# Eight gate tiles instead of four in the block of seven products, four instead of eight as fillers, and the low halves of their weights on GpSimd

## The chip, the core and the metric

The kernel runs on one core of a Trainium2 chip. The metric is the device time of one execution in microseconds (us), the median of three runs. The profile is one further execution of the same program. Engines are called as in the profile: PE (TensorE), DVE (VectorE), ACT (ScalarE), POOL (GpSimd), SP (the queue that issues most DMAs).

## What is computed

One encoder layer on 512 tokens of width 2048, in float32. One input projection gives queries, keys, values and gates of two groups of 16 heads (group A: dilated sliding windows with a bucketed bias; group B: neighbourhoods on an 8 by 64 grid). The attention outputs are multiplied by SiLU of the gates, projected once, added to a scaled input and normalised:

```python
h = jnp.einsum('bsd,de->bse', x, w_in[layer])
qa, ka, va, ga, qb, kb, vb, gb = jnp.split(h, splits, axis=-1)
ya = _dilated_attention(heads(qa, N_HEADS_A), heads(ka, N_HEADS_A), heads(va, N_HEADS_A), t5_bias)
yb = _neighbourhood_attention(heads(qb, N_HEADS_B), heads(kb, N_HEADS_B), heads(vb, N_HEADS_B), na_rpb[layer])
ya = merge(ya) * jax.nn.silu(ga.astype(jnp.float32))
yb = merge(yb) * jax.nn.silu(gb.astype(jnp.float32))
y = jnp.concatenate([ya, yb], axis=-1).astype(x.dtype)
out = jnp.einsum('bse,ed->bsd', y, w_out[layer])
x = _layer_norm(DEEPNORM_ALPHA * x + out, ln_gain[layer], ln_bias[layer])
```

The gates have 2048 columns, cut into sixteen tiles of 128 columns.

## The kernel before, in words

Every product of float32 matrices is made of three matmuls. Each operand is split into a high half, which is its copy rounded to the matmul's type (`wh`, by ACT), and a low half, which is what is left (`wl` = raw - high, by DVE); PE adds high by high, high by low and low by high.

The work runs in five stages.

1. `plain_block` computes the first `EARLY` = 4 gate tiles while the input is loaded and split.
2. `run_blocks` computes the projections of q, k and v by Strassen's scheme: a product of 2 by 2 blocks by seven products instead of eight. There are six such blocks of 28 "jobs" (7 products by 4 units). A job has four parts, issued at fixed distances: add two raw weight pieces (DVE, L371), high half (ACT, L375), low half (DVE, L380), 12 matmuls of 512 columns (PE, L402 to L404). After the fourth block stands one more block, of kind "s", for `MID` = 4 gate tiles. There the weights are the stationary side and the tokens the moving side, cut into halves of 256 tokens, so its matmuls have 256 columns (L393 to L395); it has 14 jobs of 24 such matmuls.
3. The remaining eight gate tiles and half of the output projection are "fillers": matmuls handed out one at a time by a generator. A gate tile is 48 filler matmuls of 512 columns (L561); the first half of the output projection (`out_first`, L755) is 384 more. 49 fillers run before attention starts.
4. Attention is a loop over 136 steps n, four for each of 32 heads, on the order written in the code. Heads go in pairs of group A and pairs of group B. A step makes the scores of 128 queries (PE L665 and L666), adds the bias and takes the minimum `mn` (DVE `s`, L622), takes exponentials with their sums (ACT, L626); two steps later the probabilities are transposed (PE L685 into `pt`) and split into `th` (ACT, L690) and `tl` (DVE, L691). In step n % 4 = 2 the previous head's values are multiplied in (PE L707 into `pv`: first `th`, then `tl`), and its two halves are added by way of a copy `tmp` (ACT L831) into `y` (DVE L832). Between these stand the fillers: `amount` of them in each of the four steps of a head, 8+6+1+6 = 21 up to step 63, 8+7+1+7 = 23 after that. For each pair of heads, DVE also multiplies `y` by the gates (L730) and by the reciprocal of the sums (L738) and makes the low half of `yk` (L740); the reciprocals go through memory on POOL's queue (L721, L723).
5. The second half of the output projection and the normalisation.

The fillers' weights are loaded by SP (L540) into a ring of four, asked for one piece ahead (`prepare`), split one step later (ACT L546) and two steps later (DVE L547), and used 24 matmuls at a time. The filler generator may only reach a part of `out_first` when the `yk` tile that it multiplies has been made, two for each quarter of the weights.

The order on PE, SP, DVE and ACT in stages 2 to 4 is that of the code; POOL's order is set by a scheduler.

Of the kernel before, what the change touches and what calls it, by code (L numbers as in the profile page):

```python
# [25 lines left out]
HALF = 256  # L26
# [38 lines left out]
ORDER = [(m % 2, m // 2) for m in range(2 * PAIRS)]  # L65
EARLY, MID = 4, 4
BIAS = ((0, 24), (192, 32), (448, 24))
# [3 lines left out]
def hybrid_layer(tc, xT, xn, w_in, w_early, w_mid, w_gate, w_out, t5x, brow, rpb, cmask, eye, gain, lbias, out):  # L71
    nc = tc.nc
    from contextlib import ExitStack
    with ExitStack() as ctx:
# [275 lines left out]
        def strassen_block(src, kind, g, hooks):  # L350

            base = len(jobs)
            units, tiles = (2, 1) if kind == "s" else (4, 2)

            def load(q, tags):
                def run():
                    for u in range(units):
                        raw = slot(tags[u], F32, "braw")
# [6 lines left out]
            def product(i, pool, q, other=None, onto=None):  # L365
# [7 lines left out]
                def high(u):  # L373
                    h = halves.next("wh", F32R)
                    nc.scalar.activation(h, raws[q][u], AF.Copy)  # L375
                    return h

                def low(u, h):
                    l = halves.next("wl", F32R)
                    nc.vector.tensor_tensor(l, raws[q][u], f(h), ALU.subtract)  # L380
                    return h, l

                def run(u, h, l):
                    if u == 0 and first:
                        accs.extend(bank(pool, "acc") for _ in range(tiles))
                    if kind == "s":
                        for kk in range(4):
                            k = 4 * u + kk
                            ah, al = operand(i, k)
                            for n in range(2):  # L390
                                c = slice(256 * kk + 128 * n, 256 * kk + 128 * n + 128)
                                o = accs[0][:, HALF * n:HALF * n + HALF]
                                nc.tensor.matmul(o, h[:, c], ah, start=first and k == 0 and n == 0, stop=False, skip_group_check=skip)  # L393
                                nc.tensor.matmul(o, h[:, c], al, start=False, stop=False, skip_group_check=skip)
                                nc.tensor.matmul(o, l[:, c], ah, start=False, stop=k == 7 and n == 1, skip_group_check=skip)  # L395
                    for t in range(2 if kind != "s" else 0):
# [24 lines left out]
            def pair(name):  # L421
                if name not in made:
                    t = temps.next(name)
                    made[name] = [t[:, :512], t[:, 512:]]
                return made[name]
# [46 lines left out]
            def put(name, ch, half, t):  # L472
                o = p1[t] if name == "c11" else pair(home[name])[t]
                if kind == "v":
                    store_v(g, ch, half, t, o)
                    return
                sg = vst.next("sg")[:, :512]
                silu(sg, o)
                for n in range(2):
                    nc.sync.dma_start(sg_d[EARLY + 2 * ch + n][:, HALF * half:HALF * half + HALF], sg[:, HALF * n:HALF * n + HALF])  # L480

# [54 lines left out]
        def prepare():  # L536

            while stream and len(raws) < 4:
                raws.append(raw_ring.next("wraw"))
                nc.sync.dma_start(raws[-1], stream.pop(0))  # L540
            if not raws:
                return
            raw = raws.pop(0)
            h, l = halves.next("wh", F32R), halves.next("wl", F32R)
            ready.append((h, l))
            later(1, lambda: nc.scalar.activation(h, raw, AF.Copy))  # L546
            later(2, lambda: nc.vector.tensor_tensor(l, raw, f(h), ALU.subtract), True)  # L547

# [256 lines left out]
        with tc.manual_schedule(engines=engines):  # L805
# [212 lines left out]
def _weights(w_in, w_out):  # L1018
# [20 lines left out]
    for i in range(2):  # L1039
        for j in range(2):  # L1040
            a = np.concatenate([w[8 * i:8 * i + 8, :, c:c + 128] for c in gate[EARLY + 2 * j:EARLY + 2 * j + 2]], axis=2)
            mid.append(a.reshape(2, 4, 128, 256).transpose(0, 2, 1, 3).reshape(2, 128, 1024))
    return (np.concatenate(blocks), early, np.concatenate(mid), np.concatenate([narrow(c) for c in gate[EARLY + MID:]]),
# [37 lines left out]
```

## Time and profile before

| | us |
|---|---|
| median of three runs | 976.12 (976.05 to 976.37) |
| the profiled execution, whole | 976.42 |
| its span, first to last instruction | 974.6 |
| block "s" (first to last of its matmuls) | 367.9 to 409.0 |
| first filler, first score matmul, last score matmul | 563.1, 576.4, 869.4 |

Busy shares over the span are PE 99%, DVE 78%, ACT 51%, POOL 18%. A matmul's record includes the time until its result has landed, and matmuls overlap, so PE's price for one is the distance between the starts of two neighbours and not the duration in the record. A row of a view by stretches gives the stretch, its length, and for each engine the busy time and, in brackets, the number of instructions; then the clock granted to PE, the DMA engines' busy share and their rate. A row of the view by instructions in time gives start, duration, engine, line, operation, output<-input, shape and count, and in square brackets the idle time ahead with what ended it.

### The profile page before, as it was taken

Reading aid. Unit: us, or ns where it says so; the run is one execution under the profiler, and the core shown is the slowest. Engines: PE = TensorE matmul, PEld = TensorE weight load, DVE = VectorE, ACT = ScalarE, POOL = GpSimd, SP = SyncE. Lnnn points to the kernel's source line nnn. Section 1 sums busy time; section 2 is a strip of 40 time slices with the busy share of each in tenths; the row PEclk is TensorE's granted clock in tenths of the full one; section 3 lists DMA queues with packets and bytes.
Section 4 is the critical chain, followed back from the end, with each engine's and each line's share of the span. In section 5 each row is a group of like instructions: output and inputs, shape, how many; then the busy total and the mean of one; then the engine's idle time right before and its main releaser. Section 6 shows DMA issues by size and latency. Waiting matters only on the chain.

```text
span 974.6 us, 13969 instructions
## 1 busy us (share of the span) xinstructions
PE 964.0 (99%) x4779; PEld 804.2 (83%) x4779; DVE 758.6 (78%) x1143; ACT 497.1 (51%) x858; POOL 176.5 (18%) x325
## 2 busy tenths in 40 slices
PE   8999999999999999999999999999999999999996
PEld 6887888888888889988888888888888888888885
DVE  7897778679789777796788856777876767777877
ACT  7454444444444344443445446767766666763300
POOL 1006646835642000000000000011110000100021
PEclk9999999999999999999999999999999999999998
DMA  9816796698496087420872687878877688768222
GB/s 332 280 65 133 225 329 213 171 308 220 115 334 226 22 283 204 163 96 21 265 183 96 205 273 213 226 224 228 233 229 222 195 236 214 203 223 298 87 72 102
DMA packets 119287, 194.17 MB, mean 199 GB/s; under 512 B 48479, under 2 KB 68831, under 8 KB 119216
## 3 DMA queue, kind: packets, MB, share of 16 engines
q1 hardware_dynamic: 106544, 169.67, 57.0%
q0 software_dynamic: 12096, 22.95, 8.7%
q8 instruction: 38, 0.62, 0.3%
q10 hardware_dynamic: 576, 0.66, 0.2%
q14 instruction: 33, 0.27, 0.1%
HBM read 148.68 MB, written 44.50 MB: 198 GB/s over the span
## 4 chain that ended last, share of the span: by engine, by line
PE 96%; DVE 1%; ACT 1%; DMA 1%; issue 0%; SPq 0%; DVEq 0%; ACTq 0%
PE acc L402 16%; PE acc L404 16%; PE acc L403 16%; PE acc L755 15%; PE acc L561 9%; PE pv L707 4%; PE pt L685 4%; PE sc L666 2%; PE sc L665 2%; PE pt L259 1%; PE acc L278 1%; PE acc L279 1%; PE acc L280 1%; PE sc L755 1%; PE acc L393 1%; PE acc L395 1%
## 5 line engine op out<-in xcount | busy, mean ns | idle before, releaser
L375 ACT ACTIVATE wh<-braw 128x1024 fp32r<-128x1024 f32 x182 | 193.3, 1062 | 268.6 <-PE acc L403 201.4
L380 DVE TENSOR_TENSOR wl<-braw,wh 128x1024 fp32r<-128x1024 f32 x182 | 222.7, 1226 | 52.4 <-ACT wh L375 52.1
L402 PE MATMUL acc<-wh,xk 128*128 128x512 f32 x384 | 151.5, 394 | 0.0
L404 PE MATMUL acc<-wl,xk 128*128 128x512 f32 x384 | 149.9, 390 | 0.0
L403 PE MATMUL acc<-wh,xk 128*128 128x512 f32 x384 | 149.7, 390 | 0.0
L371 DVE TENSOR_TENSOR braw<-braw 128x1024 f32<-128x1024 f32 x104 | 127.7, 1228 | 0.1
L402 PE MATMUL acc<-wh,op 128*128 128x512 f32 x288 | 113.3, 393 | 0.0
L404 PE MATMUL acc<-wl,op 128*128 128x512 f32 x288 | 112.3, 390 | 0.0
L403 PE MATMUL acc<-wh,op 128*128 128x512 f32 x288 | 112.2, 390 | 0.0
L755 PE MATMUL acc<-wh,yk 128*128 128x512 f32 x320 | 108.2, 402 | 0.0
L691 DVE TENSOR_TENSOR tl<-pt,th 128x256 fp32r<-128x256 f32 (+1 forms) x128 | 71.1, 555 | 35.8 <-ACT th L690 34.1
L690 ACT ACTIVATE th<-pt 128x256 fp32r<-128x256 f32 (+1 forms) x128 | 62.2, 489 | 47.6 <-PE pt L685 45.4
L404 PEld LDWEIGHTS acc<-wl,xk 128*128 128x128 f32 x384 | 72.1, 188 | 15.3
L402 PEld LDWEIGHTS acc<-wh,xk 128*128 128x128 f32 x384 | 72.2, 188 | 15.2 <-ACT bias L150 0.9
L403 PEld LDWEIGHTS acc<-wh,xk 128*128 128x128 f32 x384 | 72.2, 188 | 14.4
L626 ACT ACTIVATE p<-s,mn 128x512 f32<-128x512 f32 (+1 forms) x96 | 62.2, 648 | 29.0 <-DVE mn L622 28.6
L622 DVE CUSTOM_DVE_ANT_0 s<-sc,biases 128x512 f32<-128x512 f32 (+2 forms) x128 | 67.7, 529 | 10.9 <-PE sc L666 10.0
L561 PE MATMUL acc<-xk,wh 128*128 128x512 f32 x256 | 75.3, 404 | 0.0
L755 PEld LDWEIGHTS acc<-wh,yk 128*128 128x128 f32 x320 | 58.5, 189 | 8.8
L160 POOL DMA_DIRECT2D bias<-rows_d x128 | 61.3, 487 | 16.4 <-DMA bias<-rows_d 5.3
L755 PE MATMUL acc<-wl,yk 128*128 128x512 f32 x160 | 64.0, 403 | 0.0
L404 PEld LDWEIGHTS acc<-wl,op 128*128 128x128 f32 x288 | 54.1, 188 | 11.4
(185 smaller groups left out, 1707.1 us busy)
## 6 DMA issues: line engine op xcount, KB each, us to landing
braw<-in_w_in SPq DMA_DIRECT2D x96, 512.0 KB
wraw<-in_w_out SPq DMA_DIRECT2D x32, 512.0 KB
k_d<-kst SPq DMA_DIRECT2D x64, 128.0 KB
q_d<-kst SPq DMA_DIRECT2D x64, 128.0 KB
v_d<-vst SPq DMA_DIRECT2D x32, 256.0 KB
q<-q_d SPq DMA_DIRECT2D x32, 256.0 KB
wraw<-in_w_gate SPq DMA_DIRECT2D x16, 512.0 KB
k<-k_d SPq DMA_DIRECT2D x16, 512.0 KB
```

The source lines that it names most:

```text
L371: nc.vector.tensor_tensor(raws[q][u], raws[q][u], raws[other][u], ALU.add)
L375: nc.scalar.activation(h, raws[q][u], AF.Copy)
L380: nc.vector.tensor_tensor(l, raws[q][u], f(h), ALU.subtract)
L402: nc.tensor.matmul(accs[t], ah[:, q], h[:, c], start=first and k == 0, stop=False, skip_group_check=skip)
L403: nc.tensor.matmul(accs[t], al[:, q], h[:, c], start=False, stop=False, skip_group_check=skip)
L404: nc.tensor.matmul(accs[t], ah[:, q], l[:, c], start=False, stop=k == 7, skip_group_check=skip)
L561: nc.tensor.matmul(acc, w[:, k * 128:k * 128 + 128], X[8 * u + k][:, s], start=u == 0 and n == 0 and k == 0, stop=u == 1 and n == 2 and k ...
L622: nc.vector.tensor_tensor_reduce(*flat, bias, 1.0, 3e38, ALU.add, ALU.min, mn)
L626: nc.scalar.activation(p[:, to:to + n].rearrange("p (b r c) -> p b r c", r=8, c=c), s[:, :n].rearrange(order, r=8, c=c), AF.Exp, bias=mn, ...
L690: nc.scalar.activation(th, pt[:, :nch], AF.Copy)
L691: nc.vector.tensor_tensor(tl, pt[:, :nch], f(th), ALU.subtract)
L755: nc.tensor.matmul(acc[:, part], yk[k][:, s, c], w[:, wk], start=first and kk == 0 and n == 0, stop=last and kk == 1 and n == 2)
```

## The change

`MID` goes from 4 to 8. The block "s" now has four column tiles in each half of its weights instead of two: 28 jobs of 24 matmuls of 256 columns, the same job count and the same loading scheme as the other blocks, and two accumulators for each product where it had one. Four gate tiles (192 filler matmuls, eight weight pieces of 512 KB) disappear from the fillers. The low halves of the fillers' first eight weight pieces, which are all that the four remaining gate tiles use, are subtracted by POOL in two halves of 512 columns. The fillers handed out in a head's four steps become 5+3+1+2 = 11 up to step 75 and 8+6+1+6 = 21 after that. The diff, cut:

```diff
-EARLY, MID = 4, 4
+EARLY, MID = 4, 8
...
-            units, tiles = (2, 1) if kind == "s" else (4, 2)
+            units, tiles = 4, 2
+            cols, wide = (128 * MID // 2, (512, HALF * (MID // 2 - 2))) if kind == "s" else (512, (512, 512))
...
                     if kind == "s":
-                        for kk in range(4):
-                            k = 4 * u + kk
+                        for kk in range(2):
+                            k = 2 * u + kk
                             ah, al = operand(i, k)
-                            for n in range(2):
-                                c = slice(256 * kk + 128 * n, 256 * kk + 128 * n + 128)
-                                o = accs[0][:, HALF * n:HALF * n + HALF]
-                                nc.tensor.matmul(o, h[:, c], ah, start=first and k == 0 and n == 0, stop=False, skip_group_check=skip)
+                            for n in range(MID // 2):
+                                c = slice(cols * kk + 128 * n, cols * kk + 128 * n + 128)
+                                o = accs[n // 2][:, HALF * (n % 2):HALF * (n % 2) + HALF]
+                                nc.tensor.matmul(o, h[:, c], ah, start=first and k == 0 and n % 2 == 0, stop=False, skip_group_check=skip)
...
-            if kind == "s":
-                for q, ahead, i, m in ((0, 6, 0, 0), (1, 5, 0, 2), (3, 3, 1, 0), (2, 0, 1, 2)):
-                    behind.setdefault(base - ahead, []).append(load(q, tags[i][m:m + 2]))
-            else:
-                for q, ahead, i in ((0, 6, 0), (1, 4, 1), (3, 2, 2)):
-                    behind.setdefault(base - ahead if base else -4, []).append(load(q, tags[i]))
-                at(2, 2, load(2, tags[1]))
+            for q, ahead, i in ((0, 6, 0), (1, 4, 1), (3, 2, 2)):
+                behind.setdefault(base - ahead if base else -4, []).append(load(q, tags[i]))
+            at(2, 2, load(2, tags[1]))
...
-            later(2, lambda: nc.vector.tensor_tensor(l, raw, f(h), ALU.subtract), True)
+
+            def low(n):
+                c = slice(512 * n, 512 * n + 512)
+                nc.gpsimd.tensor_tensor(l[:, c], raw[:, c], f(h[:, c]), ALU.subtract)
+
+            if len(stream) + len(raws) >= 16:
+                for n in range(2):
+                    later(2, lambda n=n: low(n))
+            else:
+                later(2, lambda: nc.vector.tensor_tensor(l, raw, f(h), ALU.subtract), True)
...
-                amount = ((8, 6, 1, 6) if n < 64 else (8, 7, 1, 7))[b]
+                amount = ((5, 3, 1, 2) if n < 76 else (8, 6, 1, 6))[b]
```

What this does to the order shows at three places. First PE in the second head of attention (a head of group A), from the scores of its step n % 4 = 2; `pv` are the previous head's values, `pt` the transposes, `acc` the fillers. Before:

```order
L665 MATMUL sc<-k,q 128x512
L666 MATMUL sc<-k,ql 128x512
L707 MATMUL pv<-th,vv 128x512 x4
L707 MATMUL pv<-tl,vv 128x512 x4
L561 MATMUL acc<-xk_110,wh 128x512
L685 MATMUL pt<-ident,p 128x128 x4
L665 MATMUL sc<-k,q 128x512
L666 MATMUL sc<-k,ql 128x512
L561 MATMUL acc<-xk_111,wh 128x512
L561 MATMUL acc<-xk_112,wh 128x512
L561 MATMUL acc<-xk_113,wh 128x512
L685 MATMUL pt<-ident,p 128x128 x4
```

The same place after the change (lines are seven higher there):

```order
L672 MATMUL sc<-k,q 128x512
L673 MATMUL sc<-k,ql 128x512
L714 MATMUL pv<-th,vv 128x512 x4
L714 MATMUL pv<-tl,vv 128x512 x4
L568 MATMUL acc<-xk_102,wh 128x512
L692 MATMUL pt<-ident,p 128x128 x4
L672 MATMUL sc<-k,q 128x512
L673 MATMUL sc<-k,ql 128x512
L568 MATMUL acc<-xk_103,wh 128x512
L692 MATMUL pt<-ident,p 128x128 x4
```

Between the scores of the next step and the transposes that follow them stands one filler instead of three; the other steps are thinned in the same way.

Second DVE, from the addition `y` in the third head (L832 before, L839 after). Before:

```order
L832 TENSOR_TENSOR y<-pv,tmp 64x512
L691 TENSOR_TENSOR tl<-pt,th 128x256
L547 TENSOR_TENSOR wl<-wraw,wh 128x1024
L622 ISA s,mn<-sc,biases 128x192
L622 ISA mn 128x1
L691 TENSOR_TENSOR tl<-pt,th 128x256
```

After:

```order
L839 TENSOR_TENSOR y<-pv,tmp 64x512
L698 TENSOR_TENSOR tl<-pt,th 128x256
L629 ISA s,mn<-sc,biases 128x192
L629 ISA mn 128x1
L698 TENSOR_TENSOR tl<-pt,th 128x256
```

The low half of a filler weight, which stood between two steps' work, is gone from DVE's line.

Third POOL, from its first instruction after the setup for attention; `sg_d` are finished gate tiles, `rc_d` and `rc` the reciprocals on their way through memory. Before:

```order
L568 DMA sg_d<-sgo 128x512
L721 DMA rc_d<-tmp 8x128
L568 DMA sg_d<-sgo 128x512
L723 DMA rc<-rc_d 64x512 x2
L721 DMA rc_d<-tmp 8x128
L723 DMA rc<-rc_d 64x512 x2
```

After:

```order
L548 TENSOR_TENSOR wl<-wraw,wh 128x512 x6
L575 DMA sg_d<-sgo 128x512
L548 TENSOR_TENSOR wl<-wraw,wh 128x512 x4
L728 DMA rc_d<-tmp 8x128
L730 DMA rc<-rc_d 64x512 x2
L548 TENSOR_TENSOR wl<-wraw,wh 128x512 x2
L728 DMA rc_d<-tmp 8x128
L575 DMA sg_d<-sgo 128x512
L730 DMA rc<-rc_d 64x512 x2
```

The subtractions now share POOL's line with the issues of those DMAs; three of the eight weight pieces come ahead of the first gate's store.

More of the change, by code (lines that the diff above doesn't have):

```diff
@@ L357, in run @@
                     for u in range(units):
[L358 removed]
+                        raw = slot(tags[u], F32, "braw")[:, :2 * cols]
                         nc.sync.dma_start(raw, src[units * q + u])
@@ L373, in high @@
                 def high(u):
-                    h = halves.next("wh", F32R)
+                    h = halves.next("wh", F32R)[:, :2 * cols]
                     nc.scalar.activation(h, raws[q][u], AF.Copy)
@@ L378, in low @@
                 def low(u, h):
-                    l = halves.next("wl", F32R)
+                    l = halves.next("wl", F32R)[:, :2 * cols]
                     nc.vector.tensor_tensor(l, raws[q][u], f(h), ALU.subtract)
@@ L423, in pair @@
                     t = temps.next(name)
-                    made[name] = [t[:, :512], t[:, 512:]]
+                    made[name] = [t[:, :512], t[:, 512:512 + wide[1]]]
                 return made[name]
@@ L476, in put @@
                     return
-                sg = vst.next("sg")[:, :512]
+                sg = vst.next("sg")[:, :wide[t]]
                 silu(sg, o)
-                for n in range(2):
-                    nc.sync.dma_start(sg_d[EARLY + 2 * ch + n][:, HALF * half:HALF * half + HALF], sg[:, HALF * n:HALF * n + HALF])
+                for n in range(wide[t] // HALF):
+                    nc.sync.dma_start(sg_d[EARLY + MID // 2 * ch + 2 * t + n][:, HALF * half:HALF * half + HALF], sg[:, HALF * n:HALF * n + HALF])
             for t in range(tiles):
```

10 lines of the change are left out of this document (6 added, 4 removed).

## Prediction

> **What bounds the kernel now.** I read the page first, then PE's groups and neighbouring starts, then the stage of attention by stretches, by groups and by waits.
>
> ```profile
> span 974.6 us, 13969 instructions
> PE 964.0 (99%) x4779; PEld 804.2 (83%) x4779; DVE 758.6 (78%) x1143; ACT 497.1 (51%) x858; POOL 176.5 (18%) x325
> PE 96%; DVE 1%; ACT 1%; DMA 1%; issue 0%; SPq 0%; DVEq 0%; ACTq 0%
> ```
>
> PE is busy for 99% of the span and holds 96% of the chain that ended last: what shortens PE's work shortens the kernel, for as long as PE stays the one that is waited for. The stage at stake is attention's first 76 steps, 19 heads, in which the change hands out fewer fillers. Its stretch runs from the first score matmul to that of step 76:
>
> ```profile
> 576.42:749.42 173.00, 172.99 (x939) 143.91 (x938) 127.25 (x299) 120.42 (x284) 17.88 (x33) 1.00 0.81 227
> 576.42:749.42 173.00, 27.56 (x76) 14.37 (x76) 1.00 0.81 227
> ```
>
> The second row counts the L665 matmuls alone: 76 steps. PE is covered for all 173.0 us, DVE works 127.25 and ACT 120.42, the DMA engines are busy 81% of the time. So in this stage DVE has 46 us to spare and ACT 53, and what they wait for costs nothing yet:
>
> ```profile
> DVE tl L691 <- ACT th L690: 20.8, 29, 1.2
> DVE y L832 <- ACT tmp L831: 19.4, 16, 1.7
> ```
>
> **The change, part by part.** It moves work between two kinds of matmul and takes cover away from attention. PE's prices first, from the starts of neighbours in the view by time:
>
> ```profile
> 570.76 3.79 PE L561 MATMUL acc<-xk,wh 128*128 128x512 f32 x16
> 369.37 0.28 PE L393 MATMUL acc<-xk,wh 128*128 128x256 f32 x1
> ...
> 371.17 0.28 PE L393 MATMUL acc<-xk,wh 128*128 128x256 f32 x1
> ```
>
> Sixteen fillers in a row take 3.79 us, of which the last one's record is 0.39, so 15 distances of 0.2267 us. Between the two L393 starts, 1.80 us apart, lie 15 distances of matmuls of 256 columns (five triples of L393 to L395), 0.120 us each: more than half of 0.2267. *Removed:* four gate tiles of 48 fillers, 192 x 0.2267 = 43.5 us. *Added:* the block "s" does 7 x 48 = 336 matmuls of 256 columns before and 672 after, 336 x 0.120 = 40.3 us. PE's work falls by 3.2 us. Counted by columns it would fall by 12,288 of 98,304, an eighth of the 43.5, 5.4 us; the narrow matmul takes 2.2 of that back.
>
> The Trainium skill's TensorE page ("TensorE: Matmul & The Clock Gate", section Back-to-back issue gap) gives an isolated matmul 262 cycles at 256 columns and 518 at 512, 109 and 216 ns. By these figures 41.4 us would go and 36.7 come, 4.7 saved instead of 3.2; the trace's 120 and 227 ns do not agree, and I use the trace.
>
> The doubled block costs the other engines nothing on the path. It becomes like the k, q and v blocks, whose 28 jobs give PE 12 x 0.2267 = 2.72 us each where these give 24 x 0.120 = 2.88; DVE and ACT do the same three passes over 1024 columns for a job in both. One of those blocks:
>
> ```profile
> 99.30:176.00 76.70, 76.70 (x355) 63.48 (x354) 59.43 (x59) 34.09 (x39) 49.20 (x101) 1.00 0.77 248
> ```
>
> PE is covered throughout with DVE at 59.43 of 76.70. Eight more pieces of 512 KB are loaded there and eight fewer in attention.
>
> *Attention, steps 0 to 75.* Before, 16 heads x 21 + 3 x 23 = 405 fillers; after, 19 x 11 = 209. That is 196 fewer, 44.4 us, so PE alone would need 173.0 - 44.4 = 128.6 us. After step 76 nearly nothing changes: 768 - 49 - 405 = 314 fillers were left before, 576 - 49 - 209 = 318 are left after, at the 21 per head under which PE was covered before. So the question is whether DVE and ACT can do the 19 heads in 128.6 us. Their savings:
>
> ```profile
> L547 DVE TENSOR_TENSOR wl<-wraw,wh 128x1024 fp32r<-128x1024 f32 x17 | 20.7, 1217 | 0.0
> L567 DVE SCALAR_TENSOR_TENSOR sgo<-sgo,acc 128x512 f32<-128x512 f32 x8 | 5.4, 678 | 0.0
> L546 ACT ACTIVATE wh<-wraw 128x1024 fp32r<-128x1024 f32 x17 | 17.8, 1049 | 0.0
> ```
>
> 17 weight pieces were split here. After, 209 fillers ask for 8 or 9; the first four pieces are asked for before step 0, the next four go to POOL in steps 8 to 37, and the rest, 4, come back to DVE. So DVE loses 13 x 1.217 = 15.8 us and four `sgo`, 2.7: 127.25 - 18.5 = 108.8 us. ACT loses 8 x 1.049 and four tanh of 0.59: 109.7 us. Both fit into 128.6, at 85%. What counts is whether their waits shrink with PE's work. Here is one step with values in a head of group A:
>
> ```profile
> 660.50 0.60 PE L685 MATMUL pt<-ident,p 128*128 128x128 f32 x4
> 660.86 0.95 PE L561 MATMUL acc<-xk,wh 128*128 128x512 f32 x3
> 661.14 0.60 ACT L690 ACTIVATE th<-pt 128x512 fp32r<-128x512 f32 x1 [0.73 <-PE pt L685]
> 661.63 0.72 ACT L626 ACTIVATE p<-s,mn 128x512 f32<-128x512 f32 x1
> 661.64 0.39 PE L665 MATMUL sc<-k,q 128*128 128x512 f32 x1
> 661.77 0.69 DVE L691 TENSOR_TENSOR tl<-pt,th 128x512 fp32r<-128x512 f32 x1 [0.62 <-ACT th L690]
> 662.11 1.07 PE L707 MATMUL pv<-th,vv 128*128 128x512 f32 x4
> 662.38 0.68 DVE L622 CUSTOM_DVE_ANT_0 s<-sc,biases 128x512 f32<-128x512 f32 x1
> 663.01 1.07 PE L707 MATMUL pv<-tl,vv 128*128 128x512 f32 x4
> 663.29 0.71 ACT L626 ACTIVATE p<-s,mn 128x512 f32<-128x512 f32 x1
> 663.92 0.39 PE L561 MATMUL acc<-xk,wh 128*128 128x512 f32 x1
> 664.12 0.59 ACT L831 ACTIVATE tmp<-pv 64x512 f32<-64x512 f32 x1
> 664.75 0.68 DVE L832 TENSOR_TENSOR y<-pv,tmp 64x512 f32<-64x512 f32 x1 [1.08 <-ACT tmp L831]
> ```
>
> `tl` ends at 662.46 and `y` starts 2.29 us later, and no filler stands between: values, the exponential after `s`, and `tmp` do. So the 19.4 us of waits for `tmp` stay whatever PE saves. The waits for `th` are of another kind: `th` itself waited for transposes that PE reached late, behind fillers, and these may shrink. If all of them go, DVE's line is 108.8 + 19.4 = 128.2 us long, as long as PE's 128.6; if none goes, 149.0.
>
> I take the middle, because a walk through one head gives it. By the durations above, in us after the end of `tl`: `y` ends at 2.98; `tl` and `s` of the next step follow, ending at 3.6 and 4.2; another `tl` and `s` end at 4.8 and 5.4; the exponential, begun at 4.3, is read out at 5.1, the `th` behind it ends at 5.7, and the third `tl` waits for it and ends at 6.4; `s` and the last `tl` close the head at 7.9. PE's own work for it is four pairs of scores of 0.47, four groups of transposes of 0.36, values of 1.81 and eleven fillers, 5.1 + 2.5 = 7.6. Into the 7.9 still go about one multiplication of `y` per head (0.6, outside the gap before `y`), weights and reciprocals on ACT: 8.5, 0.9 more than PE. Group B has half the columns and less of this; I put it at 0.2 more than PE, an estimate, and the mean of both is 0.55 x 19 = 10.4 us. The same walk with 21 fillers gives PE 9.9, which covers it, as the trace shows. So the stage takes 139 us, 10.2 more than PE alone (0 to 20.4 are the ends).
>
> POOL's part has no row in this stage, but the normalisation has both engines at once:
>
> ```profile
> 933.86 0.74 DVE L893 SCALAR_TENSOR_TENSOR z<-z,rs,gain 128x512 f32<-128x512 f32 x1
> 934.93 1.48 POOL L904 TENSOR_TENSOR z<-z,gain 128x512 f32<-128x512 f32 x1 [47.67 <-issue]
> 935.30 1.66 DVE L893 SCALAR_TENSOR_TENSOR z<-z,rs,gain 128x512 f32<-128x512 f32 x1
> 936.50 1.62 POOL L905 TENSOR_TENSOR z<-z,gain 128x512 f32<-128x512 f32 x1
> ```
>
> A half piece takes POOL 1.5 to 1.6 us, a piece 3.1, and a piece is due only every 24 fillers, over two heads: POOL keeps up. The issues of `rc` queued behind it wait up to 3.1 us of the six steps before L738 needs them. But a DVE instruction with two inputs in SBUF, 0.74 us alone, took 1.66 beside POOL, 0.92 more. In attention only L730, L738 and L740 are such, three in eight steps, and four pieces of POOL's fall there: eight halves, perhaps two or three meetings, 0 to 2 us; I put it inside the middle above.
>
> **The sum.** 976.4 (profiled) - 43.5 + 40.3 + 10.2 = 983.4; the median lies 0.3 below that execution: 983.1 us.
>
> **The rivals.** *PE stays the bound.* The waits for `th` vanish with the fillers: DVE 128.2 and PE 128.6 interlock without loss, and the change gives its 3.2 us: 976.1 - 3.2 = 972.9, faster. For it: PE was covered to the last in heads where the walk left little. Against it: two in-order lines of equal length that wait for each other both ways. It decides if the stall stays under 1.3 us.
>
> *A small stall, or DMA as the bound.* The stage moves 39.3 MB at 227 GB/s with a share of 0.81, 140 us of work. Eight pieces fewer (4.2 MB at 227 / 0.81 = 280 GB/s) take 15 off: 125, which PE's 128.6 would make a share of 0.97. The highest that I see is
>
> ```profile
> 563.00:576.00 13.00, 13.00 (x59) 10.74 (x59) 4.95 (x6) 2.90 (x4) 0.00 (x0) 1.00 0.94 287
> ```
>
> At 0.94 the stage takes 133, 4.5 more than PE: 972.9 + 4.5 = 977.4, no change. Against it as the first bound: loads stand a head ahead.
>
> *No wait shrinks.* The stage takes 149.0: 972.9 + 20.4 = 993.3.
>
> *POOL holds DVE.* If each of the eight halves meets such a DVE instruction, 8 x 0.92 = 7.4 us come on top: 990.5. The Trainium skill's SBUF page ("SBUF — State Buffer", section Who interferes with whom) says that a DVE instruction with two SBUF inputs and a GpSimd one that reads SBUF exclude each other for the whole instruction; the 1.66 us beside 1.48 agree. By that rule every meeting is paid in full; it does not say how many there are.
>
> **How the numbers follow.** The forecast 0.47, PE stays the bound 0.22, small stall or DMA 0.15, no wait shrinks 0.10, POOL holds DVE 0.06. About 0.2% (1.9 us) can be told from no change here, so faster is the second case, 0.22, the same the third, 0.15, slower the others, 0.63. The range reaches from PE as the bound, 972.5, to all waits kept, with a meeting or two, 995.5.
>
> **What would show it.** Right: the block "s" 40 us longer with neighbours still at 0.120; the 76 steps at about 139 us instead of 173; idle time on PE there, ended by `tl`, `th` or exponentials, and DVE's waits for `tmp` still near 1 us per head; the stretch after step 76 covered as before. Wrong: 76 steps within 130 us; narrow matmuls at another distance; PE waiting for a DMA; L730 to L740 at 1.6 us.

## The result, and the profile after

| | before | after |
|---|---|---|
| median of five runs, us | 976.12 (975.86 to 976.37) | 1000.01 (999.08 to 1000.58) |
| ratio | | 1.0242 (95% interval 1.0231 to 1.0253) |
| span of the profiled execution, us | 974.6 | 998.7 |
| first score matmul, us | 576.4 | 616.3 |
| attention's steps 0 to 75, us | 173.0 | 153.8 |
| from step 76 to the end, us | 225.2 | 228.6 |

Slower by 2.4%. The forecast was 983.1 with a range up to 995.5: the sign was right, the size was not, and the time lies above the range. First the page of after: its span, PE's share and the chain that ended last:

```profile
span 998.7 us, 14338 instructions
...
PE 973.2 (97%) x4923; PEld 810.1 (81%) x4923; DVE 769.8 (77%) x1154; ACT 505.7 (51%) x865; POOL 205.2 (21%) x337
...
PE 84%; DMA 4%; ACT 3%; issue 3%; DVE 3%; POOL 1%; SPq 0%; DVEq 0%; ACTq 0%; POOLq 0%
```

Before, PE held 96% of the chain; now 16% of the span belongs to others, DMAs first. The doubled block is as forecast. Its narrow matmuls, in the view by instructions in time (start, duration):

```profile
371.79 0.28 PE L394 MATMUL acc<-xk,wh 128*128 128x256 f32 x1
...
373.59 0.28 PE L394 MATMUL acc<-xk,wh 128*128 128x256 f32 x1
```

1.80 us for 15 distances: 0.120 again. The first score comes 39.9 us later than before (forecast 40.3). What differs is attention. By stretches, the 76 steps and what follows them:

```profile
616.29:770.08 153.79, 139.41 (x743) 109.21 (x741) 109.49 (x282) 110.38 (x272) 28.08 (x39) 0.98 0.82 222
770.09:998.60 228.51, 219.66 (x1108) 181.31 (x1108) 171.08 (x335) 109.18 (x236) 21.55 (x29) 0.98 0.59 180
```

PE alone needs 128.6 us for the 76 steps, so the stall is 25.2 us where 10.2 was forecast. DVE's busy time is 109.5 (forecast 108.8), ACT's 110.4 (109.7). The work was counted rightly; the waits were not. Waits of these 76 steps (who waited for whom: us in total, times, longest):

```profile
DVE y L839 <- ACT tmp L838: 23.4, 18, 2.1
...
DVE tl L698 <- ACT th L697: 9.2, 21, 1.1
DVE y L745 <- DMA rc<-rc_d: 9.0, 4, 6.0
...
PE pt L723 <- DVE den L850: 4.3, 5, 2.3
...
PE sc L672 <- DMA q<-q_d: 2.7, 1, 2.7
```

The first two the forecast had (19.4, and half of 20.8). The third was 0.8 us before and has no term in the sum: DVE waits for the reciprocals. The worst of these four waits, in the chain that ended last (start, duration) and then by time:

```profile
728.95 8.85 DMA rc_d<-tmp
...
738.61 7.63 DMA rc<-rc_d
```

```profile
738.08 1.05 POOL L730 DMA_DIRECT2D rc<-rc_d  x2 [8.60 <-DMA rc_d<-tmp]
...
740.22 0.47 PE L672 MATMUL sc<-k,q 128*128 128x512 f32 x1 [2.71 <-DMA q<-q_d]
...
746.34 0.69 DVE L745 TENSOR_TENSOR y<-y,rc 128x512 f32<-128x512 f32 x1 [5.98 <-DMA rc<-rc_d]
...
748.23 0.27 PE L723 MATMUL pt<-ident,den 128*8 128x128 f32 x1 [2.29 <-DVE den L850]
```

The row of sums leaves for memory at 728.95, and DVE goes on with what came back at 746.34, 17.4 us later; this way out and back is called the trip below. DVE stands in front of its multiplication for 5.98 us, with everything that ACT and PE need from it queued behind; PE then waits for a reciprocal, 2.29. In before the first trip already held DVE for a moment:

```profile
600.88 0.54 POOL L721 DMA_DIRECT2D rc_d<-tmp  x1 [21.50 <-ACT tmp L720]
...
613.42 0.69 DVE L738 TENSOR_TENSOR y<-y,rc 128x512 f32<-128x512 f32 x1 [0.58 <-DMA rc<-rc_d]
```

The eight trips of these heads took 8.0 to 13.0 us there, from the first issue to the last landing, and two of them made DVE wait. In after seven of the eight took 7.6 to 12.8 us, no longer than before, but four made DVE wait: it is the cover that shrank. During the longest, the stretch 728 to 748 has a DMA share of 1.03 (near 1, or a little over it, the engines are full throughout):

```profile
728.00:748.00 20.00, 14.51 (x68) 10.98 (x68) 10.11 (x29) 8.97 (x26) 1.58 (x3) 0.91 1.03 248
```

PE's idle time can cost a second time. Six stretches of 3.41 us; the third column from the right is the clock granted to PE:

```profile
645.40:648.81 3.41, 1.63 (x9) 0.86 (x8) 2.26 (x8) 2.31 (x6) 0.00 (x0) 1.00 1.03 287
648.81:652.23 3.42, 3.42 (x14) 3.12 (x15) 2.54 (x6) 3.35 (x8) 1.90 (x2) 0.50 0.98 240
737.56:740.97 3.41, 0.47 (x1) 0.19 (x1) 2.76 (x6) 1.21 (x5) 1.05 (x2) 1.00 1.01 294
740.97:744.39 3.42, 3.16 (x9) 2.48 (x10) 0.00 (x0) 0.38 (x1) 0.00 (x0) 0.50 1.06 263
744.39:747.80 3.41, 1.55 (x8) 0.93 (x6) 1.46 (x4) 0.13 (x1) 0.00 (x0) 1.00 1.04 266
747.80:751.21 3.41, 2.74 (x18) 2.28 (x19) 2.48 (x8) 3.11 (x9) 0.53 (x1) 1.00 0.54 120
```

After the first and the third, in which PE has little to do, it runs at half its clock for one stretch. By half of their length the two spells lose 3.4 us, an estimate; before has none in its 76 steps. Not every such stretch is followed by one: in the fifth PE is busy for only 1.55 us, and the clock stays whole. The first spell comes just behind a trip that held DVE for 1.77 us (at 645.16). The idle time ahead of the second was ended by the load of `q`, before DVE stood in front of the reciprocals; that it belongs to the trip is said only by the first run below, in which both are gone.

### The profile page after: what moved, and what is told of

It is laid out like the page before. It is cut to its first block, busy times and chain, and to the rows that moved or that the text cites. A ratio compares the mean times of both kernels' runs of the same rounds, so it can differ in the third digit from the quotient of the medians.

```text
span 998.7 us, 14338 instructions
## 1 busy us (share of the span) xinstructions
PE 973.2 (97%) x4923; PEld 810.1 (81%) x4923; DVE 769.8 (77%) x1154; ACT 505.7 (51%) x865; POOL 205.2 (21%) x337
## 4 chain that ended last, share of the span: by engine, by line
PE 84%; DMA 4%; ACT 3%; issue 3%; DVE 3%; POOL 1%; SPq 0%; DVEq 0%; ACTq 0%; POOLq 0%
PE acc L404 15%; PE acc L406 15%; PE acc L405 15%; PE acc L762 13%; PE pv L714 3%; PE acc L394 3%; PE acc L396 3%; PE acc L395 3%; PE pt L692 2%; PE acc L568 2%; DMA rc_d<-tmp 2%; DMA rc<-rc_d 1%; PE pt L259 1%; PE acc L278 1%; PE acc L280 1%
## 5 line engine op out<-in xcount | busy, mean ns | idle before, releaser
L376 ACT ACTIVATE wh<-braw 128x1024 fp32r<-128x1024 f32 x196 | 208.1, 1062 | 291.5 <-PE acc L405 202.8
L381 DVE TENSOR_TENSOR wl<-braw,wh 128x1024 fp32r<-128x1024 f32 x196 | 242.1, 1237 | 61.6 <-ACT wh L376 61.4
L372 DVE TENSOR_TENSOR braw<-braw 128x1024 f32<-128x1024 f32 x112 | 136.4, 1218 | 0.0
L406 PEld LDWEIGHTS acc<-wl,op 128*128 128x128 f32 x288 | 54.1, 188 | 11.4
L405 PEld LDWEIGHTS acc<-wh,op 128*128 128x128 f32 x288 | 54.1, 188 | 11.0
```

Source lines behind the costliest of these rows:

```text
L372: nc.vector.tensor_tensor(raws[q][u], raws[q][u], raws[other][u], ALU.add)
L405: nc.tensor.matmul(accs[t], al[:, q], h[:, c], start=False, stop=False, skip_group_check=skip)
L406: nc.tensor.matmul(accs[t], ah[:, q], l[:, c], start=False, stop=k == 7, skip_group_check=skip)
```

## The experiments

Each ran on the same chip as the kernel before, which took 976.3 to 977.0 there; ratios are to it, with their intervals. "PE alone" for a head is its length in before less the ten fillers that it loses (2.27 us; twelve and 2.72 in the last three heads), and the stall is what a head or stage takes over that. The diffs are cut.

**The trip (e1_no_trip)**, on after: the reciprocals' DMAs are left out and a tile of ones is multiplied in, so the attention output is not divided by its sums.

```diff
-                nc.gpsimd.dma_start(rc_d[i], row)
-                for a in range(2):
-                    nc.gpsimd.dma_start(rc[64 * a:64 * a + 64], _view(rc_d, ...))
-                rcs[i] = rc
+                rcs[i] = ones
```

> The changed kernel, but the reciprocals of the softmax sums no longer travel through memory: the two kinds of POOL DMAs (sums out, rows back) are left out and the outputs of attention are multiplied by ones, so they are not normalised. Theory T (the trip): in the thinned stage the trip of two DMAs, queued behind loads, sets when DVE goes on; its 9.0 us of waits for rc and what stands behind them go, and 76 steps take 141 to 145 us instead of 153.8, the whole 987 to 991. Rival C (chain): the line DVE-ACT-PE is as long without the trip, the waits move to tmp, th and scores, and the whole stays within 3 us of 1000.

Measured 989.7 us, 1.0134 (1.0119 to 1.0149). Its 76 steps:

```profile
615.83:759.97 144.14, 135.74 (x744) 106.97 (x742) 109.38 (x282) 110.15 (x272) 14.79 (x14) 1.00 0.79 224
```

This is theory T. The steps are 9.65 us shorter than after's, with the same work on DVE, no half clock and no wait of PE for `q`. Of the stall of 25.2 this is the trip with all that goes when it goes, 3.4 of half clock included; 15.6 remain. The run also takes the trip's 2.0 MB off the DMA engines; e12 below leaves them in and comes to the same length.

**POOL's low parts (e2_lows_dve)**, on after: all low parts of the fillers' weights on DVE.

```diff
-            if len(stream) + len(raws) >= 16:
-                for n in range(2):
-                    later(2, lambda n=n: low(n))
-            else:
-                later(2, lambda: nc.vector.tensor_tensor(l, raw, f(h), ALU.subtract), True)
+            later(2, lambda: nc.vector.tensor_tensor(l, raw, f(h), ALU.subtract), True)
```

> The changed kernel with all low halves of filler weights on DVE again. Four more pieces of 1.22 us in DVE's line within the 76 steps. Theory D (DVE's line is what counts): up to 4.9 us longer, 1000 to 1005. Rival P (POOL hurts: subtractions of 2.5 us ahead of the reciprocals' DMAs, and DVE's two-input instructions held): 2 to 6 us shorter, 994 to 998.

Measured 999.88, 1.0233 (1.0215 to 1.0251): neither theory's range.

```profile
615.89:770.49 154.60, 139.46 (x744) 108.68 (x742) 113.74 (x287) 109.71 (x272) 15.52 (x29) 0.98 0.80 221
```

DVE has 4.2 us more to do and the stage is 0.8 longer. So work on DVE is not by itself time, and POOL's part does no harm that counts.

**Thin fillers without the doubled block (e3_before_thin)**, on before: after's amounts up to step 43, the fillers that this leaves handed out later.

```diff
-                amount = ((8, 6, 1, 6) if n < 64 else (8, 7, 1, 7))[b]
+                amount = ((5, 3, 1, 2) if n < 44 else (9, 7, 1, 7) if n < 80 else (8, 6, 1, 6))[b]
```

> The kernel before, with four gate tiles in the block of seven and all low halves on DVE, and only the number of fillers changed: 11 per head in the first 11 heads, 24 in the next nine, 21 after that, 88 behind attention. All of PE's work is kept. The first eleven heads took 99.6 us before, 110 fillers less make 74.6 for PE alone; they took 83.7 after the change. Theory A (thinning alone is the cause): 82 to 88 us for the eleven heads, the whole 984 to 990. Rival (POOL's subtractions or the wider block of seven are the cause): at most 77 us and at most 979.

Measured 989.18, 1.0126 (1.0109 to 1.0143). The first eleven heads in before, in this run and in after:

```profile
576.43:675.97 99.54, 99.53 (x537) 82.52 (x536) 72.01 (x169) 69.00 (x162) 9.79 (x18) 1.00 0.80 226
```

```profile
576.44:661.54 85.10, 78.76 (x427) 61.39 (x426) 64.27 (x162) 62.84 (x155) 8.64 (x16) 1.00 0.79 229
```

```profile
616.29:699.95 83.66, 78.77 (x428) 63.11 (x426) 60.35 (x157) 63.44 (x155) 21.18 (x26) 0.98 0.83 236
```

110 fillers fewer should save 24.9 us; 14.4 come. This is theory A: the thinning makes the stall, not the block or POOL.

**More fillers in the steps, fewer ahead (e4_more_early)**, on after:

```diff
-PROLOGUE = 10
+PROLOGUE = 4
...
-                amount = ((5, 3, 1, 2) if n < 76 else (8, 6, 1, 6))[b]
+                amount = ((6, 3, 1, 3) if n < 76 else (8, 6, 1, 6))[b]
```

> The changed kernel with the 49 fillers ahead of attention cut to 7, and 13 fillers per head instead of 11 in the 76 steps. PE's work is the same in all. Theory A (PE is not what the stage waits for): 38 more fillers of 0.227 us fit into the idle time of the 76 steps, which stay at 150 to 156 us, while the stretch ahead of them shrinks by 42 x 0.227 = 9.5 us: the whole 989 to 993. Rival (the waits add to PE's work, whatever it is, as a trip of fixed length would): the 76 steps grow by 8.6 us and the whole stays at 998 to 1001.

Both theories miss: measured 1007.07, 1.0312 (1.027 to 1.0354). Attention starts 6.2 us earlier, before its values have arrived, as the chain shows, and half clock costs 8.1 us in the 76 steps, again by half of its length. The fillers ahead of step 0 had covered loads, so the run says nothing on the amounts.

```profile
618.27 6.33 DMA vv<-v_d
```

**The waits for `tmp` (e5_y_late)**, on after: `y` is added behind the next step's `s`.

```diff
-                    nc.vector.tensor_tensor(y, mine, t, ALU.add)
+                    held.append(lambda y=y, mine=mine, t=t: nc.vector.tensor_tensor(y, mine, t, ALU.add))
```

> The kernel after, with the addition y (pv + tmp) issued one step later, behind the next step's bias addition s, so that tmp has long been copied when DVE reaches it. Theory W: DVE's line (its busy time plus the 23.4 us that it waits for tmp) is what holds the 76 steps, so these waits go and the stage falls from 153.8 us to 140 to 146 (PE's 128.6, the reciprocals' trip of about 10, a few us for th): 986 to 992 us in all. Rival: the wait only changes places, because PE waits for the bank that y empties or ACT for the next tile; the stage stays above 150 and the time at 996 or more.

Measured 1013.45, 1.0372 (1.0347 to 1.0396): the rival's side, far above its bounds. Waits of the 76 steps (163.2 us):

```profile
DVE tl L698 <- ACT th L697: 45.3, 42, 2.6
...
PE sc L672 <- DVE mn L629: 18.2, 18, 2.4
```

DVE's wait for `tmp` is gone and two others have grown: 45.3 us for `th`, and 18.2 on PE. Scores and `pv` share two banks of PSUM, the memory that PE writes to. With `y` late, `pv` keeps one of them for longer, and all 18 waits are at the first scores of a head, which go on when `s` has read the scores before them (`mn`). Theory W, that DVE's busy time plus its waits is the length of the stage, falls: here a wait showed where DVE's spare time lay, not what held the stage.

**The multiplication four steps later (e6_mult_late)**, on after, and **both moves (e7_both_late)**:

```diff
-                if n >= 8 and n % 8 == 7:
-                    gated(i - 1)
+                if n >= 19 and n % 8 == 3:
+                    gated(i - 2)
+                if n == 135:
+                    gated(i - 1)
```

(The thin amounts last until step 79 here.)

> The kernel after, with the multiplication of y by the reciprocals and the two yk steps behind it moved four steps later, nothing left out; the reciprocals go the same way through memory. Theory T: the loss of about 10 us that went when the trip was left out was DVE waiting for a transfer that came late, so more time for it does the same: 987 to 992 us, no wait of DVE for rc. Rival: it was the trip's own work (its issues on POOL, its packets among the loads, the copy by ACT), which stays: 996 or more.

> Both moves together on the kernel after. If W and T are both right and add up, hardly a wait of DVE stays in the 76 steps but those for th (9 us): DVE 109.5 + 9 is under PE's 128.6, so PE is the bound again, the stage takes 129 to 136 us and the whole 973 to 981. Rival: another chain (the DMA engines at a share of 0.94, or the ring from PE by ACT and DVE back to PE within a step) holds the stage at 140 or more: 985 or more.

Measured 1001.01, 1.0233 (1.0204 to 1.0261), and 1020.19, 1.0445 (1.0419 to 1.0472): by their times, the rivals. In the first no wait of DVE for `rc` is left in the 76 steps and they take 148.8 us, 5.0 less, about half of what e1 gained; what keeps the other half was not found. Ten fillers more behind the last score (2.3 us) and a trip that is late there give it back, as the chain shows:

```profile
888.41 7.10 DMA xl<-in_xn
...
895.55 7.20 DMA rc<-rc_d
```

The second run adds the losses of the `y` move: its 76 steps take 166.2 us.

**The order of the loads (e9_kq_later)**, on after: `if n % 8 == 0 and n < 120` ahead of `load_kq(i + 1)` becomes `n % 8 == 2`.

> The kernel after, with the loads of the next pair's k, q and ql issued two steps later (n % 8 == 2 instead of 0), so that the reciprocals' trip, which starts at n % 8 == 1, is issued ahead of them. Theory Q: the trip comes late because its packets stand behind these loads; ahead of them it is in time, DVE no longer waits for rc, and most of the 10 us goes: 989 to 994 us. Rival: the DMA queues are full all the time, so the delay only changes over to k and q, for which PE then waits: 997 or more.

Measured 1001.39, 1.0258 (1.0228 to 1.0289): the rival's time.

```profile
DVE y L745 <- DMA rc<-rc_d: 6.1, 4, 2.9
...
DVE s L629 <- DMA biases<-biasb_d: 2.3, 1, 2.3
...
PE sc L672 <- DMA q<-q_d: 1.7, 2, 1.0
```

The trip is still late, and biases and `q` as well. So it is not these loads alone that stand in front of it.

**The multiplications on POOL (e10_pool_mult), with the loads of e9 (e12_pool_mult_kq)**, on after; POOL then waits for `rc`, and the two `yk` steps behind come two steps later:

```diff
-            nc.vector.tensor_tensor(yp, yp, sgs[i]..., ALU.mult)
+            nc.gpsimd.tensor_tensor(yp, yp, sgs[i]..., ALU.mult)
...
-            later(0, lambda: nc.vector.tensor_tensor(y, y, rcs[i], ALU.mult), True)
+            later(0, lambda: nc.gpsimd.tensor_tensor(y, y, rcs[i], ALU.mult))
```

> The kernel after, with both multiplications of y (by the gates and by the reciprocals) on POOL instead of DVE, and the two yk steps behind them two steps later. It is POOL that waits for rc now. Theory W (DVE's line holds the heads that are longer than PE alone): DVE gives up 2 x 0.68 us for each of 9 pairs, 12.3 us, and the wait for rc; the stage falls from 153.8 to 132 to 138 us and the whole to 978 to 985. Rival: the heads are held by the ring of latencies inside a step (scores, s, exponential, transposes, th, tl, values, tmp, y), in which these multiplications hardly stand: only the 10 us of the trip go, 988 to 992.

> The two edits of the runs before together, multiplications on POOL and the loads of k, q and ql two steps later. If POOL already hides the trip, the order of the loads is worth nothing more: within 2 us of the run with the multiplications alone. If PE had been waiting for k, q or ql there, or the trip still held something, 3 us or more apart.

Measured 991.04, 1.015 (1.0128 to 1.0171), and 990.37, 1.0143 (1.0127 to 1.0158): the rival's time, and no difference between them. The 76 steps of e12:

```profile
615.61:759.75 144.14, 135.24 (x744) 106.65 (x742) 102.67 (x265) 108.85 (x271) 49.16 (x55) 1.00 0.85 235
```

The same 144.1 us as without the trip (e10 takes 145.55, with one spell of half clock). 17 DVE instructions of 0.68 us are gone, 11.6 us, but DVE's busy time fell only by 6.8. Groups of after, then of e12:

```profile
L554 DVE TENSOR_TENSOR wl<-wraw,wh 128x1024 fp32r<-128x1024 f32 x4 | 4.9, 1214 | 0.0
```

```profile
L554 DVE TENSOR_TENSOR wl<-wraw,wh 128x1024 fp32r<-128x1024 f32 x4 | 6.8, 1708 | 0.0
...
L747 DVE SCALAR_TENSOR_TENSOR yk<-y,yk 128x512 fp32r<-128x512 f32 x7 | 6.6, 938 | 0.0
```

DVE's instructions with both inputs in SBUF got longer beside POOL's (`yk` 0.69 in after), as the Trainium skill's SBUF page ("SBUF — State Buffer", section Who interferes with whom) has it.

**A bank of its own for `pv` (e14_own_bank), and `y` late with it (e15_own_bank_y_late)**, on e12, in the first twelve heads:

```diff
-            pv = bank(pss, "pv")
+            pv = at_bank(3, "pv") if h < 12 else bank(pss, "pv")
```

(The fourth accumulator bank; a gate tile's fillers then take turns on three.)

> The kernel with the multiplications on POOL and the loads of k, q and ql two steps later (144.1 us for the 76 steps, 15.5 over PE alone), and in its first twelve heads pv has a PSUM bank of its own, so that the scores find both of theirs. Heads 4 to 11 took 61.2 us there; PE alone would need 54.0. Theory B (the scores' wait for the bank that y empties is what closes the ring): these eight heads fall to 54 to 57 us, and the whole by 4 to 7 us, 983 to 986. Rival L (the ring of latencies from scores to values within a head, whatever the bank): 60 us or more, and the whole stays at 988 to 992.

> As the run with pv in a bank of its own, and y is added one step later in the first eleven heads with values, behind the next step's s; the bank that made this edit slower by itself is out of the way. Theory B: the wait of DVE for tmp goes there without a new one, heads 4 to 11 are at 54 to 56 us, 1 to 3 less than with the bank alone. Rival L: the wait for tmp is only where DVE's spare time shows; within 1 us of the run with the bank alone, or longer.

Measured 996.13, 1.0204 (1.0179 to 1.0229), and 998.73, 1.0233 (1.022 to 1.0246): slower, on the rival's side. Attention starts 4.6 us later, and heads 4 to 11 take 62.9 us instead of 61.2, because head 5 takes 12.7. In it one DVE instruction, 0.69 us long in after, stands between two of POOL's, and a spell of half clock follows at 659.61:

```profile
654.10 1.30 POOL L556 TENSOR_TENSOR wl<-wraw,wh 128x512 fp32r<-128x512 f32 x1
...
654.99 2.75 DVE L755 SCALAR_TENSOR_TENSOR yk<-y,yk 128x512 fp32r<-128x512 f32 x1
...
655.88 1.29 POOL L745 TENSOR_TENSOR y<-y,sg 128x512 f32<-128x512 f32 x1
```

The even heads tell something cleaner. Heads 8 and 10, in e12 and here:

```profile
672.86:679.97 7.11, 7.07 (x41) 5.68 (x41) 4.57 (x15) 5.59 (x15) 1.83 (x2) 1.00 0.87 282
...
689.14:696.24 7.10, 7.06 (x42) 5.61 (x40) 4.53 (x15) 5.48 (x15) 1.83 (x2) 1.00 0.89 263
```

```profile
678.93:685.73 6.80, 6.80 (x41) 5.62 (x40) 4.85 (x15) 5.81 (x17) 1.84 (x2) 1.00 0.70 236
695.20:702.11 6.91, 6.91 (x41) 5.72 (x40) 4.36 (x14) 5.27 (x15) 1.82 (x2) 1.00 0.82 246
```

PE alone is 6.82. So the bank is what these heads still lacked, but it is worth 0.2 to 0.3 us each. With `y` late too (e15) these two heads take 6.78 and 6.90: the wait for `tmp` is worth nothing.

**All of a finished pair on POOL (e16_pair_on_pool), the gate weights' high halves too (e17_highs_on_pool)**, on e12:

```diff
-            later(3, lambda: nc.scalar.activation(t[:, 0], y, AF.Copy, scale=0.5))
-            later(4, lambda: nc.vector.scalar_tensor_tensor(t[:, 1], y, 0.5, f(t[:, 0]), ...), True)
+                nc.gpsimd.tensor_copy(t[:, 0], y)
+                nc.gpsimd.tensor_tensor(t[:, 1], y, f(t[:, 0]), ALU.subtract)
...
+            if len(stream) + len(raws) >= 16:
+                later(1, lambda: nc.gpsimd.tensor_copy(h, raw))
```

(The last two lines are e17's; both have the factor 0.5 in the reciprocals.)

> All that is done to a finished pair on POOL: both multiplications, the high half of yk (before on ACT) and its low half (before on DVE; the factor 0.5 goes into the reciprocals), with the loads of k, q and ql two steps later. Beside the run with the multiplications and the loads alone (144.1 us for the 76 steps, 15.5 over PE), ACT loses 9 x 0.62 us and DVE 9 x 0.69. Theory E (it is not the mean that counts: in single heads, the second and fourth of each four, ACT's or DVE's work is over PE's, 8.3 to 8.6 against 8.0 and 6.4 against 5.4): these heads shorten, the stage takes 136 to 140 us and the whole 982 to 986. Rival L (latencies inside a head): 142 or more, 988 to 991.

> As the run before, and the high halves of the gate fillers' weights are also made by POOL (8 pieces, 8.4 us off ACT). Theory E: another 1 to 4 us less in the 76 steps. Rival L: within 1 us, or longer, since POOL has now more to do beside DVE.

Measured 992.68, 1.0157 (1.0097 to 1.0218), and 989.28, 1.0132 (1.0085 to 1.018). The four runs of each lie up to 12 us apart, so the medians decide nothing; e16's is above both theories' ranges. The profiled execution of e17 is the fastest of its four. Its 76 steps take 140.2 us, 4.0 under e12 and at the upper end of what theory E had for e16:

```profile
615.97:756.15 140.18, 134.27 (x744) 106.68 (x742) 96.03 (x258) 101.54 (x259) 67.20 (x74) 1.00 0.87 245
```

In that of e16 the odd heads 5 to 13 shorten as in e17 (1.2 us in 5 and 7, 0.6 in 9, 11 and 13, against e12), but a load of 9.83 us stops PE in heads 15 and 16 (11.4 and 9.9 us, two spells of half clock):

```profile
727.44 9.83 DMA ql<-q_d
```

Lengths of heads 8 to 11 in us, by stretches from first score to first score:

| | 8 | 9 | 10 | 11 |
|---|---|---|---|---|
| before | 9.09 | 10.27 | 9.09 | 7.63 |
| PE alone with 11 fillers | 6.82 | 8.00 | 6.82 | 5.36 |
| after | 7.17 | 9.20 | 7.97 | 6.13 |
| no trip (e1) | 7.38 | 9.16 | 7.45 | 6.14 |
| multiplications on POOL (e12) | 7.11 | 9.17 | 7.10 | 6.81 |
| with a bank for `pv` (e14) | 6.80 | 9.47 | 6.91 | 6.51 |
| all of the pair and the high halves on POOL (e17) | 7.11 | 8.59 | 7.11 | 6.20 |

**Six gate tiles instead of eight**, 16 fillers to a head up to step 75: alone (e8_six_tiles), with the multiplications on POOL (e11_six_pool), with the loads of e9 as well (e13_six_pool_kq), and with all of the pair on POOL (e18_six_pair_on_pool).

```diff
-EARLY, MID = 4, 8
+EARLY, MID = 4, 6
...
-                amount = ((5, 3, 1, 2) if n < 76 else (8, 6, 1, 6))[b]
+                amount = ((7, 4, 1, 4) if n < 76 else (8, 6, 1, 6))[b]
```

> The kernel after with six gate tiles in the block of seven products and six as fillers, 16 fillers to a head up to step 75 instead of 11. PE saves half of its 3.2 us. Theory W (the longer of two lines): PE needs 128.6 + 95 x 0.227 = 150.2 us for the 76 steps, DVE's line with four more low parts, two more gate tiles and 32 us of waits about 148: nearly equal, so a stall of 1 to 6 us, part of the trip among it: 976 to 981 us. Rival: each filler taken away costs its share of the stall of 25 us: half of it, 12: 986 to 988.

> Six gate tiles in the block of seven products, 16 fillers to a head up to step 75, and both multiplications of y on POOL. PE alone would give 1.6 us. Theory W: with 16 fillers PE needs 150.2 us for the 76 steps and DVE's line is now some 14 us shorter than that of the run with six tiles before (stall 9.5 us there, over 5 of it in one head that waits for the trip): a stall of 0 to 3 us is left: 975 to 979 us, beside 976 before the change. Rival: the stall is one of latencies inside the steps and stays at 4 to 5 us: 980 to 982.

> Six gate tiles, the multiplications on POOL, and the loads of k, q and ql two steps later. With 16 fillers to a head a stall of 2.7 us was left in the 76 steps without the third edit. If part of it is the trip or the loads, it falls to 1 to 2 us: 976 to 977, level with the kernel before the change. Rival: it is the heads' own ring: 977.5 to 978.5.

> Six gate tiles with all that is done to a finished pair on POOL. With the multiplications alone on POOL the 76 steps took 152.8 us, 2.7 over PE, and the whole 977.9. Theory E: the rest of the stall goes, 976 to 977. Rival L: 977.5 to 979.

Measured 988.26, 1.0116 (1.009 to 1.0141); 977.86, 1.0017 (1.0008 to 1.0027); 978.53, 1.0029 (1.0017 to 1.0041); 975.45, 0.999 (0.998 to 0.9999). The first and the third lie just above their rivals' ranges, the second in theory W's (by its number; e5 had ruled out what W says), the last a little under theory E's. The 76 steps of the first and the last, where PE alone needs about 150:

```profile
596.17:755.79 159.62, 154.23 (x838) 125.71 (x837) 113.92 (x286) 115.81 (x278) 40.03 (x49) 0.99 0.85 233
```

```profile
596.11:747.40 151.29, 151.26 (x839) 124.53 (x837) 97.56 (x260) 111.19 (x270) 72.36 (x78) 1.00 0.88 239
```

The stall of 9.5 us in the first (over 5 of it in head 18) shrinks to about 1 when POOL takes over the pair and waits for the trip. In that last version the DMA engines are as full for 20 us as they were in after, and PE does not stop:

```profile
728.00:748.00 20.00, 20.00 (x110) 16.33 (x109) 14.62 (x34) 15.05 (x35) 3.41 (x4) 1.00 1.05 228
```

It is level with before within the 0.2% that can be told; nothing tried beats before by more.

## Why the forecast missed

*PE's prices, the block, DVE's and ACT's work.* Right: 0.120 us, 39.9 for 40.3, 109.5 for 108.8, 110.4 for 109.7.

*"The issues of `rc` queued behind it wait up to 3.1 us of the six steps before L738 needs them."* This step failed, with "loads stand a head ahead" in the DMA rival. Both put the slack in steps or heads, and a step is not a time: 173.0 / 76 = 2.28 us before, 128.6 / 76 = 1.69 by PE alone after. Six steps shrink from 13.7 to 10.2 us, while a trip took up to 13.0 before and up to 17.3 after. The sum put it at nothing, although before's own rows had DVE waiting for it; e1 puts it at 9.65 us in the 76 steps, and 10.3 on the whole (1000.0 less 989.7).

*The DMA rival.* It asked whether the mean share would come to 0.94; the mean is 0.82. But the share comes in bursts: 728 to 748 is at 1.03, and there the prediction's own sign of being wrong appears, PE waiting 2.71 us for a load. (Nor is 0.94 the highest in before: stretches of 4 us there reach 1.06, 708 to 712 for one.) That the bursts made the longest trip long is argued, not tested. e9 shows that this order of the loads does not help, and e18 that DMA engines as full as this cost nothing where nothing on PE's way waits for them.

*"Group B has half the columns and less of this; I put it at 0.2 more than PE, an estimate"*. This second step failed too; it had no row. Without the trip (e1), the ten heads of group A take 6.0 us more than PE alone, 0.60 each (0.9 in the walk), the nine of group B 9.6, 1.07 each: A took 3.0 us less than its 9.0, B 7.8 more than its 1.8. The difference, 4.8, is nearly all of the 5 us by which the stage without the trip is still over the forecast. e14 gives 0.2 to 0.3 of a head's excess to the bank that `y` frees. e17, without the pair's steps on ACT and DVE, is 4.0 shorter in the stage than e12, nearly all of it in odd heads; part of that only undoes what e12 had lengthened there (head 11). What holds the rest is not settled. The other way to 139 in the prediction, DVE's work plus its waits (108.8 + 19.4 + half of 20.8), met the walk by chance: with 4.2 us more work on DVE (e2) the stage grew by 0.8, with 6.8 less (e12) it was as long as without the trip, and without the wait for `tmp` (e5) it grew.

*The waits for `th`, and "no wait shrinks".* The halving was right, 9.2 for 10.4. The waits for `tmp` grew from 19.4 to 23.4 instead of staying.

*"POOL holds DVE."* Not here: L737 went from 0.68 to 0.82 us on the mean over eight instructions, 1.1 us in all and nearly all of it in one (1.78), and e2 shows no loss. The prediction's list of DVE instructions with two inputs in SBUF lacked the low halves `wl` (L547 there); in e12 these lengthened most, from 1.21 to 1.71 on the mean.

*After step 76.* "Covered as before" holds but for 2.5 us (228.6 against 225.2 + 0.9 for four fillers more). In e1 it is 1.3; what that is was not tested.

So the miss of 17 us is about 10 of trip (3.4 of that half clock), 5 of the heads (group B) and 2 at the end. The first is shown by leaving the trip out and by moving the wait to POOL, though e6, which only gives the trip more time, won about half of it in the stage; of the second the size is shown and the cause only in part.

## What to carry to other kernels

Before shortening a stage, list what in it has a fixed duration (trips through memory, loads) and compare it with the time of the steps that cover it after the change, not with their number. Read an engine's margin head by head and the DMA share in stretches of a few us; a mean of 0.82 had 20 us at 1.03 in it. Where engines wait for each other in a circle, a wait in the profile is not a price: in e5 23.4 us of waits were taken away, and the kernel got 13 us slower.

## What the hardware showed besides

A stall of PE can cost more than its length. Each spell of half clock in after's 76 steps lasts 3.413 us and costs half of that, 1.71, where PE has work throughout. The two start 92.16 us apart, 27 times 3.413, and the five of e5 start 11, 13, 5 and 6 such lengths apart: they begin on a fixed beat. The Trainium skill's TensorE page ("TensorE: Matmul & The Clock Gate", section What's actually happening) states this beat, a free-running window of 3413 ns, and the trace agrees. Its table speaks of an idle window; here a window with nine matmuls and 1.63 us of PE busy in 3.41 was enough, and no single wait of PE for others in after was over 2.71 us. Another window, with eight matmuls and 1.55 us, was not followed by a spell, so these runs give no threshold. e5, with its five spells, lost 8.5 us by them, by the same half.
